# Queries and keys of a head pair leave PSUM in one cast and one subtraction; on-chip copies fill the stacks

## The chip, the core and the metric

The kernel runs on one core of one Trainium2 chip. Five engines work side by side, each through its own queue in order: PE (TensorE, matrix products), DVE (VectorE) and ACT (ScalarE) for elementwise work, POOL (GpSimd), and SP (SyncE), which here only issues DMA transfers. They wait for one another through semaphores. The metric is the time of one execution on the device in microseconds (us).

## The reference

One layer of a decoder: a half-step feed-forward block, two attention branches over one input projection, their gated sum, and a second half-step feed-forward block. Sequence 512, width 1024, everything in float32.

```python
x = x + 0.5 * swiglu_ffn(x, g1, wg1, wu1, wd1)
h = rms_norm(x, mix_norm)
(fq, fk, fv, ff, dq, dk, dv, iq, ik, iw, ga, gb) = split_columns(h @ w_in)
fq = rms_norm(fq.reshape(B, S, 8, 64), fox_q_norm)     # per head
fk = rms_norm(fk.reshape(B, S, 8, 64), fox_k_norm)
o_a = fox_attention(fq, fk, fv, log_sigmoid(ff + b_forget))
dq = rms_norm(dq.reshape(B, S, 8, 64), dsa_q_norm)
dk = rms_norm(dk, dsa_k_norm)                          # one key head for all
o_b = dsa_attention(dq, dk, dv, iq, ik, iw, rel_bias)  # top-128 keys
x = x + (sigmoid(ga) * (o_a @ wa) + sigmoid(gb) * (o_b @ wb)) @ w_out
x = x + 0.5 * swiglu_ffn(x, g2, wg2, wu2, wd2)
```

Branch A (FoX) has 8 query heads and 8 key heads of 64 columns. Branch B (DSA) has 8 query heads and one shared key head.

## The kernel before

Matrix products are made from two parts of each float32 number, a rounded high part (dtype fp32r) and the rest, the low part: high = cast(x), low = x - high. A product is the sum of three such products (`mm3`, lines 132 to 135). For the scores of attention there is a shorter form, since a head has only 64 columns and the array has 128 rows. A *stack* holds the high part of a head's queries in 64 partitions and the low part in the other 64, for all 512 positions. The keys lie twice, in `kh` (high, in both halves) and `kl` (low, in both halves). Two products, stack by `kh` and stack by `kl` (`stack_mm`, lines 651 and 652), then give all four terms.

The sequence of work in the middle part of the kernel is a loop over 16 heads `g`: 0 to 7 are FoX, 8 to 15 DSA. Each head has four beats `s`, one for each block of 128 queries, from the last block to the first. In a beat PE turns a block column of probabilities of the head before (`flip`, line 924: transposes into the PSUM bank `pt`; ACT casts it into `ph`, line 928, and DVE subtracts into `pl`, line 929), weighs values with it (`weigh`, lines 934 and 935, into `po`), makes the scores of the present block (`ps_qk`), and then a fixed amount of projection products (`ps_t`, `ps_f`) as filling. DVE adds the bias to the scores and takes the minimum (line 913), ACT takes the exponential (line 915), POOL divides (line 917). Between these DVE also makes steps of a top-128 search (`topk`, lines 861 to 866), which may only stand behind anchors: the instructions handed to `mark`.

Queries and keys of a pair of heads are prepared during the odd head ahead of the pair: `get_q(g + 1)` in beat 0 and, for FoX, `get_k(g + 1)` in beat 1. Four transposes (line 626) bring the 128 columns of both heads to the partitions of one PSUM bank, `ps_q` or `ps_k`: the even head in partitions 0 to 63, the odd head in 64 to 127. Both banks come from the tag `pt` with two buffers, which the transposes of line 924 use too. `split_own` then treats each head by itself: ACT scales and casts 64 partitions (line 645), DVE subtracts 64 partitions (line 646), and for queries these two write straight into the two halves of the head's stack, `st`. For keys the two parts of a head are written to the head's own half, and SP copies each to the other half by a DMA (line 978). The keys are the tiles `kh` and `kl`, three buffers each; the stacks have two buffers.

SP's queue carries, in order, the weight loads (line 122), the copies of keys (line 978) and the bias tile of the next head, `cb` (line 984: a row of cumulative forget sums spread over 128 partitions; two buffers, so that the load for head g + 1 waits until head g - 1 has read its own). The order of PE is the order of the program; the order of the other queues is set by a scheduler that simulates the kernel.

The function `evac_split` (lines 608 and 609), which casts and subtracts 128 partitions at once, is used for the shared key head of branch B.

## Time and profile before

| | us |
|---|---|
| median of 3 runs (1090.44 to 1095.73) | 1091.22 |
| the profiled execution | 1087.2 |
| its span, from the first to the last instruction | 1085.5 |

| engine | busy us | share of the span | instructions |
|---|---|---|---|
| PE, matrix products | 1069.2 | 99% | 6880 |
| DVE | 794.6 | 73% | 1286 |
| ACT | 575.9 | 53% | 908 |
| POOL | 194.4 | 18% | 248 |

How to read it: times in rows are microseconds from the start of the span. In a timeline row the first number is the start, the second the duration; in brackets stands how long the engine sat idle before the instruction and what released it. The queries and keys are prepared between 417 and 618 us. The granted clock of PE is 1.00 in every stretch of this time.

### The profile page before, as it was taken

Reading aid. Unit: us, or ns where it says so; the run is one execution under the profiler, and the core shown is the slowest. Engines: PE = TensorE matmul, PEld = TensorE weight load, DVE = VectorE, ACT = ScalarE, POOL = GpSimd, SP = SyncE. Lnnn points to the kernel's source line nnn. Section 1 sums busy time; section 2 is a strip of 40 time slices with the busy share of each in tenths; the row PEclk is TensorE's granted clock in tenths of the full one; section 3 lists DMA queues with packets and bytes.
Section 4 is the critical chain, followed back from the end, with each engine's and each line's share of the span. In section 5 each row is a group of like instructions: output and inputs, shape, how many; then the busy total and the mean of one; then the engine's idle time right before and its main releaser. Section 6 shows DMA issues by size and latency. Waiting matters only on the chain.

```text
span 1085.5 us, 17835 instructions
## 1 busy us (share of the span) xinstructions
PE 1069.2 (99%) x6880; PEld 966.8 (89%) x6880; DVE 794.6 (73%) x1286; ACT 575.9 (53%) x908; POOL 194.4 (18%) x248
## 2 busy tenths in 40 slices
PE   9999999999999999998999999999999999999998
PEld 7889899988998899988878778889998899989997
DVE  6895578755967489879665765879986688865874
ACT  5553155522555676887655685455663155522650
POOL 0000000000001415565552640001110001000100
PEclk9999999999999999999999999999999999999999
DMA  7434325533442368765124221425574356633552
GB/s 244 115 98 135 108 87 148 138 96 98 115 118 85 104 128 189 184 157 117 58 65 135 80 68 40 144 83 152 140 166 141 89 136 161 161 97 101 143 126 78
DMA packets 43573, 131.01 MB, mean 121 GB/s; under 512 B 5337, under 2 KB 5721, under 8 KB 43489
## 3 DMA queue, kind: packets, MB, share of 16 engines
q1 hardware_dynamic: 35120, 107.58, 32.4%
q0 software_dynamic: 8208, 22.02, 11.9%
q8 instruction: 54, 0.88, 0.3%
q10 hardware_dynamic: 160, 0.28, 0.1%
q14 instruction: 31, 0.25, 0.1%
HBM read 117.79 MB, written 2.11 MB: 110 GB/s over the span
## 4 chain that ended last, share of the span: by engine, by line
PE 86%; DVE 5%; DMA 3%; ACT 2%; issue 2%; POOL 2%; SPq 0%; DVEq 0%; POOLq 0%; ACTq 0%
PE pd L133 7%; PE pd L135 7%; PE pd L134 7%; PE pB L133 5%; PE pB L135 5%; PE pB L134 5%; PE pC L133 3%; PE pA L133 3%; PE pA L134 3%; PE pC L135 3%; PE pC L134 3%; PE pA L135 3%; PE ps_f L133 3%; PE ps_f L134 3%; PE ps_f L135 3%; DMA cb<-cum_rows 2%
## 5 line engine op out<-in xcount | busy, mean ns | idle before, releaser
L134 PE MATMUL pd<-al,wh 128*128 128x512 f32 (+1 forms) x294 | 113.2, 385 | 0.0
L133 PE MATMUL pd<-ah,wh 128*128 128x512 f32 (+1 forms) x294 | 113.2, 385 | 0.0
L135 PE MATMUL pd<-ah,wl 128*128 128x512 f32 (+1 forms) x294 | 113.1, 385 | 0.0
L112 ACT CAST wh<-s 128x1024 fp32r<-128x1024 f32 x57 | 60.1, 1055 | 98.6 <-PE pB L134 48.4
L133 PE MATMUL pB<-tbh,wh 128*128 128x256 f32 x304 | 85.0, 279 | 0.2 <-DVE u L435 0.2
L134 PE MATMUL pB<-tbl,wh 128*128 128x256 f32 x304 | 84.8, 279 | 0.0
L135 PE MATMUL pB<-tbh,wl 128*128 128x256 f32 x304 | 84.7, 279 | 0.0
L133 PE MATMUL ps_t<-wh,xh 128*128 128x256 f32 (+1 forms) x288 | 81.0, 281 | 0.0
L134 PE MATMUL ps_t<-wl,xh 128*128 128x256 f32 (+1 forms) x288 | 80.3, 279 | 0.0
L135 PE MATMUL ps_t<-wh,xl 128*128 128x256 f32 (+1 forms) x288 | 80.3, 279 | 0.0
L113 DVE TENSOR_TENSOR wl<-s,wh 128x1024 fp32r<-128x1024 f32 x57 | 69.4, 1217 | 1.8 <-ACT wh L112 1.7
L271 POOL DMA_DIRECT2D al<-gu x26 | 22.3, 858 | 260.7 <-ACT al L270 248.6
L135 PEld LDWEIGHTS pd<-ah,wl 128*128 128x128 f32 x294 | 55.3, 188 | 11.1
L134 PEld LDWEIGHTS pd<-al,wh 128*128 128x128 f32 x294 | 55.2, 188 | 10.9
L133 PEld LDWEIGHTS pd<-ah,wh 128*128 128x128 f32 x294 | 55.2, 188 | 10.8
L393 POOL DMA_DIRECT2D s<-in_w_pair_dram x11 | 9.7, 879 | 296.1 <-DVE wl L113 296.1
L133 PEld LDWEIGHTS pB<-tbh,wh 128*128 128x128 f32 x304 | 57.1, 188 | 0.6 <-issue 0.6
L134 PEld LDWEIGHTS pB<-tbl,wh 128*128 128x128 f32 x304 | 57.2, 188 | 0.0
L135 PEld LDWEIGHTS pB<-tbh,wl 128*128 128x128 f32 x304 | 57.1, 188 | 0.0
L133 PEld LDWEIGHTS ps_t<-wh,xh 128*128 128x128 f32 x288 | 54.3, 189 | 0.5
L134 PEld LDWEIGHTS ps_t<-wl,xh 128*128 128x128 f32 x288 | 54.3, 189 | 0.5
L135 PEld LDWEIGHTS ps_t<-wh,xl 128*128 128x128 f32 x288 | 54.3, 188 | 0.0
(354 smaller groups left out, 3597.0 us busy)
## 6 DMA issues: line engine op xcount, KB each, us to landing
rc<-in_w_pair_dram SPq DMA_DIRECT2D x16, 512.0 KB, 3.6
rb<-in_w_pair_dram SPq DMA_DIRECT2D x16, 512.0 KB, 3.6
ra<-in_w_pair_dram SPq DMA_DIRECT2D x15, 512.0 KB, 3.6
rd<-in_w_pair_dram SPq DMA_DIRECT2D x15, 512.0 KB, 3.7
re<-in_w_pair_dram SPq DMA_DIRECT2D x14, 512.0 KB, 3.8
al<-gu POOLq DMA_DIRECT2D x26, 256.0 KB, 4.7
s<-in_w_pair_dram POOLq DMA_DIRECT2D x11, 512.0 KB, 5.5
ra<-in_w_down_dram SPq DMA_DIRECT2D x7, 512.0 KB, 3.6
```

What stands on the lines that cost most here:

```text
L112: S.copy(wh[:, :f], raw[:, :f])
L113: V.tensor_sub(wl[:, :f], raw[:, :f], wh[:, :f].bitcast(F32))
L133: PE.matmul(out, lh, rh, start=start, stop=False, **more)
L134: PE.matmul(out, lh, rl, start=False, stop=False, **more)
L135: PE.matmul(out, ll, rh, start=False, stop=stop, **more)
L271: G.dma_start(l, u, accum_op=OP.add)
L393: G.dma_start(t["s2"], load["b"][2], accum_op=OP.add)
```

## The change

For the first pair (g = 0) nothing changes but the order of allocation. For the seven other pairs of queries and the three other pairs of FoX keys, one cast and one subtraction over 128 partitions (`evac_split`) replace two of each over 64. [...] For queries the high parts go to the even head's stack, all 128 partitions of it, and the low parts to a scratch tile `low` from the pool `tmp` (six buffers); three copies of 64 partitions then bring the odd head's high part to its stack, the even head's low part into the second half of the even stack, over the odd head's high part, and the odd head's low part into the odd stack. The copy into the second half of the even stack must wait until the copy that reads that half has landed. For keys both parts go to the even head's tiles; for each of `kh` and `kl` two copies bring the odd head's half to both halves of the odd tile, and a third brings the even head's half over it. That third copy waits for the first two.

```diff
             out = [at.tile([P, T], F32R, tag=tag, bufs=2, name="st") for tag in ("qh", "ql")]
-            for hf, st in enumerate(out):
-                own, oth = sides(hf)
-                split_own(ps, gain, own, st[own], st[oth])
+            if g == 0:
+                for hf, st in enumerate(out):
+                    own, oth = sides(hf)
+                    split_own(ps, gain, own, st[own], st[oth])
+                return out
+            even, odd = out
+            low = tmp_tile("low").bitcast(F32R)
+            evac_split(ps, gain, even, low)
+            copy_half(odd[0:DH], even[DH:P])
+            copy_half(even[DH:P], low[0:DH])
+            copy_half(odd[DH:P], low[DH:P])
             return out
+
+        def copy_half(dst, src):
+            nc.sync.dma_start(dst.bitcast(F32), src.bitcast(F32))
...
-            out = []
-            for hf in range(2):
-                own, oth = sides(hf)
-                k = [mp.tile([P, T], F32R, tag=tag, bufs=3, name=tag) for tag in ("kh", "kl")]
-                split_own(ps, hg[:, 2:3], own, k[0][own], k[1][own])
-                for t in k:
-                    nc.sync.dma_start(t[oth].bitcast(F32), t[own].bitcast(F32))
-                out.append(k)
+            out = [[mp.tile([P, T], F32R, tag=tag, bufs=3, name=tag) for tag in ("kh", "kl")] for _ in range(2)]
+            if g == 0:
...
+            evac_split(ps, hg[:, 2:3], *out[0])
+            for even, odd in zip(*out):
+                for part in (slice(0, DH), slice(DH, P)):
+                    copy_half(odd[part], even[DH:P])
+                copy_half(even[DH:P], even[0:DH])
             return out
```

PE's instructions and their order stay the same. ACT and DVE have 10 casts and 10 subtractions fewer; SP has 43 copies in place of 16.

SP's queue while the pair of heads 2 and 3 is prepared, before. `kh_4747` and `kl_4748` are the even head's keys, `kh_4753` and `kl_4754` the odd head's; `cb_4901` is the bias of head 3.

```order
L122 DMA rb_5064<-in_w_dq_dram 128x1024
L978 DMA kh_4747<-kh_4747 64x512
L978 DMA kl_4748<-kl_4748 64x512
L978 DMA kh_4753<-kh_4753 64x512
L978 DMA kl_4754<-kl_4754 64x512
L122 DMA rc_5244<-in_w_dq_dram 128x1024
L984 DMA cb_4901<-cum_rows_3396 128x512
```

The same place of SP's queue after the change: `st_4692` is the even stack, `st_4693` the odd one, `kh_4749` and `kl_4750` are the even keys, `kh_4751` and `kl_4752` the odd ones.

```order
L122 DMA rb_5066<-in_w_dq_dram 128x1024
L975 DMA st_4693<-st_4692 64x512
L975 DMA st_4693<-low_4694 64x512
L975 DMA st_4692<-low_4694 64x512
L975 DMA kh_4751<-kh_4749 64x512 x2
L975 DMA kl_4752<-kl_4750 64x512 x2
L975 DMA kh_4749<-kh_4749 64x512
L975 DMA kl_4750<-kl_4750 64x512
L1000 DMA cb_4903<-cum_rows_3396 128x512
L122 DMA rc_5248<-in_w_dq_dram 128x1024
```

Nine copies stand where four stood, the copies that complete the even keys are the last of them, and the bias of head 3 has moved ahead of the weight load.

SP's queue at the pair of heads 6 and 7, before; `cb_5747` is the bias of head 7.

```order
L978 DMA kh_5617<-kh_5617 64x512
L978 DMA kl_5618<-kl_5618 64x512
L978 DMA kh_5623<-kh_5623 64x512
L978 DMA kl_5624<-kl_5624 64x512
L984 DMA cb_5747<-cum_rows_3396 128x512
```

And after; the even keys are `kh_5623` and `kl_5624`, `cb_5753` is the bias of head 7.

```order
L975 DMA st_5565<-st_5564 64x512
L975 DMA st_5565<-low_5566 64x512
L975 DMA st_5564<-low_5566 64x512
L975 DMA kh_5625<-kh_5623 64x512 x2
L975 DMA kl_5626<-kl_5624 64x512 x2
L975 DMA kh_5623<-kh_5623 64x512
L1000 DMA cb_5753<-cum_rows_3396 128x512
L975 DMA kl_5624<-kl_5624 64x512
```

The load of the bias, which waits until head 5 has read the tile's old content for the last time, now stands ahead of the copy that completes the even head's low keys.

DVE's queue at beat 0 and 1 of head 1, where the pair of heads 2 and 3 is prepared, as one piece of the difference. `st`, `low` and `kl` are the subtractions, `pl` that of the probabilities, the rows of lines 861 and 863 are steps of the search.

```order
-L646 SCALAR_TENSOR_TENSOR st<-ps_q,gq,st 64x512
+L609 SCALAR_TENSOR_TENSOR low<-ps_q,gq,st 128x512
+L863 MATCH_REPLACE sc_3400<-m_4709,sc_3400 128x512
+L861 MAX m_4772<-sc_3398 128x8
 L929 TENSOR_TENSOR pl<-pt,ph 128x512
 L616 TENSOR_REDUCE ss<-sqh 128x8
 L916 RECIPROCAL rs<-rs 128x1
+L609 SCALAR_TENSOR_TENSOR kl<-ps_k,hg,kh 128x512
+L863 MATCH_REPLACE sc_3398<-m_4772,sc_3398 128x256
+L861 MAX m_4823<-sc_3399 128x8
 L617 TENSOR_SCALAR ss<-ss 128x8
-L646 SCALAR_TENSOR_TENSOR st<-ps_q,gq,st 64x512
```

The subtraction that frees the bank `ps_q` is done once and early (its second half stood below `L617`, the last row here); two steps of the search, anchored on it, now stand ahead of `pl`, and the subtraction of the keys stands ahead of where its first half stood.

## The prediction

> **What bounds the kernel now.** I read the page first: busy time by engine, and the chain of work that ended last.

> ```profile
> PE 1069.2 (99%) x6880; PEld 966.8 (89%) x6880; DVE 794.6 (73%) x1286; ACT 575.9 (53%) x908; POOL 194.4 (18%) x248
> PE 86%; DVE 5%; DMA 3%; ACT 2%; issue 2%; POOL 2%; SPq 0%; DVEq 0%; POOLq 0%; ACTq 0%
> ```

> PE is busy for 99% of the span. The change takes no product away, so it can only gain PE's idle time (1085.5 - 1069.2 = 16 us, part of it at the start) or add to it. Casts and subtractions saved on ACT and DVE count only where PE waited for them. Next I read who waited for whom on PE, over the attention alone (440 to 660 us):

> ```profile
> PE pt L924 <- DVE pl L929: 1.9, 3, 0.9
> PE pt L924 <- DVE rs L916: 1.7, 2, 0.9
> PE po L935 <- DVE pl L929: 1.6, 3, 1.0
> PE pt L924 <- DVE st L646: 1.5, 2, 1.0
> PE po L934 <- DVE o L947: 1.1, 3, 0.7
> PE ps_q L626 <- POOL kn L724: 0.8, 1, 0.8
> PE pt L924 <- POOL p L917: 0.6, 2, 0.3
> PE ps_k L626 <- DVE pl L929: 0.6, 2, 0.3
> ```

> The numbers are the total, the count and the longest. All eight rows sum to 9.8 us, 0.9% of the time: this is the whole that a change to these evacuations could win, and only 1.5 us stand on the subtraction of queries itself.

> **What is removed.** The price of each old instruction, and of the new ones, which the kernel already uses once for the shared key (the numbers behind the count are the least, the median and the greatest duration in ns):

> ```profile
> L645 ACT ACTIVATE st<-ps_q,gq x16: 674/683/687, 429.7 to 617.0; 64x512 fp32r<-64x512 f32 x16
> L646 DVE SCALAR_TENSOR_TENSOR st<-ps_q,gq,st x16: 743/750/756, 431.9 to 617.9; 64x512 fp32r<-64x512 f32 x16
> L608 ACT ACTIVATE dkh<-ps_dk,hg x1: 674/674/674, 420.9 to 420.9; 128x512 fp32r<-128x512 f32 x1
> L609 DVE SCALAR_TENSOR_TENSOR dkl<-ps_dk,hg,dkh x1: 729/729/729, 423.0 to 423.0; 128x512 fp32r<-128x512 f32 x1
> ```

> 128 partitions cost what 64 cost. So seven pairs of queries and three of keys save 10 x 0.68 = 6.8 us of ACT and 10 x 0.75 = 7.5 us of DVE. Nearly all of it lies beside PE's work. What reaches PE is the bank: `ps_q` is free after one subtraction instead of two, and the transposes of the next beat find it free.

> For branch B the banks then alternate strictly: the transposes of beat 2 wait for `low` and no longer for the `pl` of the beat before. Its waits behind an evacuation are these:

> ```profile
> 534.04 0.52 PE L924 MATMUL pt<-ident,p 128*128 128x128 f32 x3 [0.77 <-DVE rs L916]
> 558.34 0.55 PE L924 MATMUL pt<-ident,p 128*128 128x128 f32 x3 [0.92 <-DVE pl L929]
> 559.54 0.50 PE L934 MATMUL po<-ph,dvv 128*128 128x512 f32 x1 [0.65 <-DVE o L947]
> L913 DVE CUSTOM_DVE_ANT_0 p<-ps_qk,b 128x384 f32<-128x384 f32 x6 | 3.3, 550 | 0.1
> ```

> At 534 (pair 8) the transposes gain up to 0.77, but the product with `pl` two instructions later needs the same `pl`, so I take 0.6. At 558 (pair 10) 0.92 goes, and what is late next is `po`, which waits for `o`; the scheduler has moved `o` ahead of one score block (0.55, last row), so 0.6 of the 1.57 goes. Pairs 12 and 14 show nothing of this size. **Branch B: -1.2 us** (bounds 0 and -2.3, the three waits).

> **What is added: a chain of copies.** The old evacuation of queries needed no DMA. Now the even stack is complete only after ACT's cast, a first copy, and a second one that waits for the first to land. For keys each copy was independent; now the even keys need copies to the odd tile first, then one more. The price of a copy from its issue to its landing, in the three stretches where FoX keys are copied (the row of the `kl` copies, then the landing of all four):

> ```profile
> L978 SPq DMA_DIRECT2D kl<-kl x2: 461/464/467, 454.2 to 455.8; - x2
> DMA to landing us min/median/max: 2.2/4.3/4.6
> L978 SPq DMA_DIRECT2D kl<-kl x2: 461/462/462, 482.8 to 485.3; - x2
> DMA to landing us min/median/max: 2.2/2.2/4.2
> L978 SPq DMA_DIRECT2D kl<-kl x2: 461/464/467, 510.7 to 513.0; - x2
> DMA to landing us min/median/max: 2.2/2.4/3.9
> ```

> A copy takes 2.2 us alone, and up to 4.6 when other transfers are in flight; issuing one holds SP for 0.46. Bounds per copy: 2.2 and 4.6.

> Queries have room. The tightest pair is the last:

> ```profile
> 613.99 0.60 PE L626 MATMUL ps_q<-ident,kn 128*128 128x128 f32 x4
> 622.63 0.39 PE L651 MATMUL ps_qk<-dkh,st 128*128 128x512 f32 x1
> ```

> Between the end of the transposes and the first use lie 8.0 us; the cast and two copies take 0.7 + 2 x 2.2 = 5.1, or 6.7 at 3.0 each. I cost the query copies at nothing; the cover is the filling products of that head, and it is gone from 3.6 us a copy on.

> Keys are made one beat later and have less. Here are the end points, for pairs 2, 4 and 6 in turn: the transposes or the subtraction that start the chain, and the product that uses the even low keys (pair 4: also a weight load and the last copy on SP; pair 6: the score block on DVE and the load of the bias):

> ```profile
> 450.67 0.63 PE L626 MATMUL ps_k<-ident,kn 128*128 128x128 f32 x4 [0.29 <-DVE pl L929]
> 459.67 0.40 PE L652 MATMUL ps_qk<-kl,st 128*128 128x512 f32 x1
> 482.02 0.74 DVE L646 SCALAR_TENSOR_TENSOR kl<-ps_k,hg,kh 64x512 fp32r<-64x512 f32 x1
> 484.58 0.33 SPq L122 DMA_DIRECT2D rc<-in_w_ga_dram  x1
> 485.27 0.46 SPq L978 DMA_DIRECT2D kl<-kl  x1
> 488.09 0.39 PE L652 MATMUL ps_qk<-kl,st 128*128 128x512 f32 x1
> 513.18 0.29 DVE L913 CUSTOM_DVE_ANT_0 p<-ps_qk,cb 128x128 f32<-128x128 f32 x1
> 513.57 0.62 SPq L984 DMA_DIRECT2D cb<-cum_rows  x1
> 515.64 0.39 PE L652 MATMUL ps_qk<-kl,st 128*128 128x512 f32 x1
> ```

> Let t be the time of one copy.

> Pair 2: `ps_k` is complete at 451.3, less the 0.29 that it waited. Cast and subtraction (0.67 + 0.73) and two handovers end at 452.9. The two copies of `kl` to the odd tile leave SP at 453.0 and 453.5, the second lands at 453.5 + t, and the last copy at 453.6 + 2t. With t = 3.6, between the least and the greatest here, that is 460.8: **1.1 us** after the present use at 459.67. The chain takes the place of the 1.0 us wait for `st`, which goes.

> Pair 4: the first subtraction ends at 482.8 today; with the second query subtraction gone but two search steps moved ahead of the scores, I leave it at 482.2. The copies leave at 482.4 and 482.9. One lands after 2.2. The last one leaves at 485.2, just behind a weight load of 512 KB, as today's last copy does, which took 4.2. So 489.4, **1.3 us** after 488.09.

> Pair 6: the scheduler has put the bias load ahead of the last `kl` copy. That load waits until head 5's last score block has read the old bias (513.18 + 0.29). SP issues the load at 513.57 and can issue the copy only at 514.2. With 2.6 for it, 516.8: **1.2 us** after 515.64.

> Who waits: PE, at the first product of heads 2, 4 and 6, with everything behind it. Behind the waiting copies on SP stand the bias of a later head and weight loads. The bias waits for the end of its head anyway, so it loses less than 1 us, and at pair 2 it gains its place ahead of a weight load; the weights have at least a beat in hand. I cost these at nothing; if a bias lands later, POOL and the softmax behind it add that lateness to the head.

> **What is absorbed.** A late PE finds its next waits shorter, where others set them. The next ones behind pairs 2, 4 and 6:

> ```profile
> 475.99 0.44 PE L626 MATMUL ps_q<-ident,kn 128*128 128x128 f32 x2 [0.82 <-POOL kn L724]
> 490.93 0.66 PE L924 MATMUL pt<-ident,p 128*128 128x128 f32 x4 [0.35 <-POOL p L917]
> 526.81 0.39 PE L935 MATMUL po<-pl,fv 128*128 128x256 f32 x1 [0.34 <-DVE pl L929]
> ```

> The first two hang on POOL, which is paced by its own queue and the biases that it waits for; the third on DVE, which now has less to do. I take all three as swallowed: 0.8, 0.35 and 0.35.

> **Sum** against the profiled execution, 1087.2: pair 2 +1.1 - 0.8 = +0.3; pair 4 +1.3 - 0.35 = +0.95; pair 6 +1.2 - 0.35 = +0.85; branch B -1.2. Together +0.9, so 1088.1. The median of the runs shown, 1091.22, stands 4.0 above the profiled execution; in its terms the forecast is 1092.1. About 0.5% (5.5 us) is what a measurement of this kernel can tell from no change, so this is within it.

> With one t for all key copies the same sum reads (2t - 6.9) + (2t - 5.4) + (t - 1.8) - 1.2 = 5t - 15.3, until a pair has no stall left.

> [...]

> **The rivals.**
> Copies land in time. Every copy takes 2.2 us, as the medians of pairs 4 and 6 nearly do. Pair 2 completes its keys at 458.0 and pair 4 at 487.4, before their use; their gains are mostly lost again in the waits that POOL sets, so about 0 each. Pair 6 still ends at 516.4, +0.4 after its absorption. With branch B -0.8: 1086.4, or 1090.4. For it: the copies could ride in quiet stretches. Against it: pair 2 runs beside a 512 KB load that POOL issues, and nine copies now follow each other.

> Slower, by the copies' contention. More copies in a row, with weight loads and POOL's loads beside them, push every copy to 4.6: 5 x 4.6 - 15.3 = +7.7, hence 1098.9. It decides from t = 4.2 on, where the sum passes +5.5. For it: the median at pair 2 is 4.3. Against it: at pairs 4 and 6 it is 2.2 and 2.4.

> Faster by relief. DVE is the engine behind most of the waits on PE; with 7.5 us fewer on it, waits elsewhere in the attention could shrink too. To pass 5.5 us it would have to clear over half of the 9.8 us and leave no stall on keys: 1085.

> **How the numbers follow.** Forecast (near balance, 1089.5 to 1096) 0.58; in time 0.21; slower by contention 0.16; relief 0.05. The first two lie within 0.5%, which makes 0.79; faster 0.05, slower 0.16. The range reaches from the in-time case with branch B at its bound and a gain of about 1 us kept at pairs 2 and 4 (1090.4 - 1.1 - 1.1 = 1088.2), 1088, to the contention case with the longest copy of the trace, 1099.

> **What would show it.** PE's waits should show new rows at lines 651 and 652 for a DMA of `kl`, `kh` or `st`, 1 to 3 us long, at the start of heads 2, 4 and 6 and nowhere else; the wait for `st` on line 924 gone; ACT and DVE 7 us less busy; the last `kl` copy of pair 6 issued right behind the bias. The forecast is wrong if heads 8 to 14 begin with such a wait, if the key copies take other than 2.2 to 4.6 us, or if PE's waits for POOL grow because a bias lands late.

## The result and the profile after

| | before | after |
|---|---|---|
| median of the runs, us | 1091.55 (4 runs) | 1105.3 (4 runs, 1102.18 to 1106.43) |
| ratio to before, 95% interval | | 1.0114 (1.008 to 1.0148) |
| the profiled execution, us | 1087.2 | 1102.18 |
| its span, us | 1085.5 | 1100.5 |

The change costs 1.1%. The forecast was 1092.1 with a range to 1099; the time lies outside it, on the slow side. The profiled execution is 15.0 us longer than that of before.

The page of the changed kernel: busy time of each engine with its share of the span.

```profile
PE 1074.9 (98%) x6880; PEld 971.7 (88%) x6880; DVE 785.1 (71%) x1276; ACT 569.2 (52%) x898; POOL 194.1 (18%) x248
```

DVE is 9.5 us and ACT 6.7 us less busy, where 7.5 and 6.8 were worked out. But the same 6880 products keep PE busy for 5.7 us longer (1069.2 before), and its idle time rose from 16.3 to 25.6 us, by 9.3. These two make the 15.0. First the idle time: the two largest rows of PE's waits over the attention (440 to 660 us; total, count, longest).

```profile
PE ps_qk L651 <- DMA kh<-kh: 6.1, 2, 4.9
PE ps_qk L652 <- DMA kl<-kl: 4.6, 3, 2.5
```

The wait for `st` on line 924 (1.5 us before) is gone, and 10.7 us of waits for copies of keys have come. PE's timeline shows where: the first two rows at head 2, the next two at head 4, the last at head 6.

```profile
461.32 0.50 PE L651 MATMUL ps_qk<-kh,st 128*128 128x512 f32 x1 [1.21 <-DMA kh<-kh]
461.98 0.50 PE L652 MATMUL ps_qk<-kl,st 128*128 128x512 f32 x1 [0.16 <-DMA kl<-kl]
496.25 0.49 PE L651 MATMUL ps_qk<-kh,st 128*128 128x512 f32 x1 [4.88 <-DMA kh<-kh]
498.70 0.79 PE L652 MATMUL ps_qk<-kl,st 128*128 128x512 f32 x1 [1.96 <-DMA kl<-kl]
530.60 0.67 PE L652 MATMUL ps_qk<-kl,st 128*128 128x512 f32 x1 [2.51 <-DMA kl<-kl]
```

Most of it, 6.84 us, stands at head 4. SP's queue there, in the changed kernel (start, time that issuing held the queue):

```profile
481.27 0.47 SPq L975 DMA_DIRECT2D st<-st  x1
482.06 5.56 SPq L975 DMA_DIRECT2D st<-low  x2
487.71 1.19 SPq L975 DMA_DIRECT2D kh<-kh  x2
488.99 1.19 SPq L975 DMA_DIRECT2D kl<-kl  x2
490.70 0.46 SPq L975 DMA_DIRECT2D kh<-kh  x1
491.21 0.58 SPq L122 DMA_DIRECT2D rc<-in_w_ga_dram  x1
492.31 1.32 SPq L975 DMA_DIRECT2D kl<-kl  x1
493.73 0.54 SPq L1000 DMA_DIRECT2D cb<-cum_rows  x1
```

The copies from the stack to the odd stack and from `low` are the queries'. The second row holds two of them: one leaves at 482.06, the other overwrites what the first copy still reads, and leaves only when that has landed. All that SP has to issue stands behind it. ACT's row for the high keys of this pair, and DVE's for the low keys:

```profile
484.39 0.69 ACT L608 ACTIVATE kh<-ps_k,hg 128x512 fp32r<-128x512 f32 x1
485.11 0.75 DVE L609 SCALAR_TENSOR_TENSOR kl<-ps_k,hg,kh 128x512 fp32r<-128x512 f32 x1 [0.42 <-ACT kh L608]
```

The high keys are ready at 485.08, and their first copy leaves at 487.71: 2.6 us in the queue. The low keys are ready at 485.86, and their first copy leaves at 488.99, 3.1 us later. How long this pair's copies took to land, first those of `st`, then those of `kh` (least, median, most):

```profile
DMA to landing us min/median/max: 2.2/4.0/5.9
```

```profile
DMA to landing us min/median/max: 2.3/2.3/5.5
```

The 5.9 is the first query copy (481.27 to 487.15, where the waiting one leaves). The 5.5 is the one that completes the even `kh`: it leaves at 490.70 and lands at 496.2, where PE's wait ends. The copy that completes the even `kl` took longer still; the chain of work that ended last shows it (start, length), and PE's second wait ends behind it:

```profile
492.31 6.35 DMA kl<-kl
```

Now the longer busy time. Windows of PE behind the three waits (from:to, length, busy time and instructions, granted clock, DMA share, GB/s):

```profile
462.50:465.50 3.00, 3.00 (x16) 0.50 0.86 171
496.60:503.20 6.60, 4.64 (x21) 0.50 0.23 69
530.80:534.10 3.30, 3.30 (x16) 0.50 0.00 0
535.00:540.00 5.00, 5.00 (x35) 1.00 0.00 0
```

Behind each of the three waits the granted clock is 0.50 for some 3.4 or 6.8 us, 13.65 us together. PE is idle for 1.96 us of them, within the second wait of head 4, and busy for 11.7 (3.00 + 4.64 + 3.30 = 10.9 in these windows, 0.75 at their edges). Nearly all that PE does there is `ps_t` products, which follow one another every 0.213 us (499.72 to 502.92 us, 15 steps); at a clock of 1.00 they follow every 0.117 (535.73 to 537.25, 13 steps). By this ratio an estimated 5.3 of the 11.7 us are lost, most of the 5.7. Before, the clock was 1.00 throughout this stretch. The profiled execution is the fastest of the four; the other three had a mean granted clock of 0.989 to 0.992 where it had 0.994, so slow stretches took more of their time.

### The profile page after: what moved, and what is told of

It reads as the page before. It is cut to its first block, busy times and chain, and to the rows that moved or that the text cites. A ratio compares the mean times of both kernels' runs of the same rounds, so it can differ in the third digit from the quotient of the medians.

```text
span 1100.5 us, 17863 instructions
## 1 busy us (share of the span) xinstructions
PE 1074.9 (98%) x6880; PEld 971.7 (88%) x6880; DVE 785.1 (71%) x1276; ACT 569.2 (52%) x898; POOL 194.1 (18%) x248
## 4 chain that ended last, share of the span: by engine, by line
PE 88%; DMA 4%; DVE 3%; ACT 2%; issue 1%; POOL 1%; SPq 0%; DVEq 0%; ACTq 0%; POOLq 0%
PE pd L133 7%; PE pd L134 7%; PE pd L135 7%; PE pB L133 5%; PE pB L135 5%; PE pB L134 5%; PE pC L133 3%; PE pC L135 3%; PE pA L133 3%; PE pA L134 3%; PE pC L134 3%; PE pA L135 3%; PE ps_f L133 3%; PE ps_f L134 3%; PE ps_f L135 3%; PE ps_t L133 2%
## 5 line engine op out<-in xcount | busy, mean ns | idle before, releaser
L134 PE MATMUL ps_t<-wl,xh 128*128 128x256 f32 (+1 forms) x288 | 82.6, 287 | 0.0
L135 PEld LDWEIGHTS pd<-ah,wl 128*128 128x128 f32 x294 | 55.2, 188 | 11.1
L133 PEld LDWEIGHTS pd<-ah,wh 128*128 128x128 f32 x294 | 55.2, 188 | 10.9
L134 PEld LDWEIGHTS pd<-al,wh 128*128 128x128 f32 x294 | 55.2, 188 | 10.7
L134 PEld LDWEIGHTS ps_t<-wl,xh 128*128 128x128 f32 x288 | 56.6, 196 | 0.6
L133 PEld LDWEIGHTS ps_t<-wh,xh 128*128 128x128 f32 x288 | 56.6, 196 | 0.4
L915 ACT ACTIVATE p<-p,mn 128x512 f32<-128x512 f32 (+1 forms) x64 | 36.0, 562 | 40.1 <-DVE mn L913 39.7
```

The costliest lines, as they stand in the source:

```text
L133: PE.matmul(out, lh, rh, start=start, stop=False, **more)
L134: PE.matmul(out, lh, rl, start=False, stop=False, **more)
L135: PE.matmul(out, ll, rh, start=False, stop=stop, **more)
L915: S.activation(p, p, AF.Exp, bias=mn, scale=-1.0, accum_out=rs)
```

## The experiments

Three candidate causes: the keys' own chain of two landings, the queries' waiting copy ahead of the keys on SP, and the mere number of copies with their contention. Beside them the question whether the clock falls because of the waits. Unless said otherwise each experiment is an edit of the changed kernel. The first four ran beside one another on a chip (before: 1090.75 us), so did the next four (1090.73) and the last two (1090.32).

| experiment | median us | ratio to before (95%) | profiled: waits for copies of keys or queries at heads 2, 4, 6 | time at half clock, 446 to 560 us |
|---|---|---|---|---|
| the change | 1105.3 | 1.0114 (1.008 to 1.0148) | 10.7 | 13.7 |
| keys alone | 1104.47 | 1.0123 (1.0105 to 1.014) | 11.1 | 13.7 |
| queries alone | 1091.29 | 1.0012 (0.9995 to 1.003) | 0 | 6.8 |
| PE kept busy | 1096.63 | 1.007 (1.0048 to 1.0092) | 0.5 | 0 |
| chain on the odd head | 1097.18 | 1.006 (1.0041 to 1.0078) | 1.0 | 13.7 |
| keys, no chain | 1089.81 | 0.9997 (0.9988 to 1.0006) | 0 | 0 |
| keys first | 1095.47 | 1.0046 (1.0029 to 1.0063) | 9.0 | 6.8 |
| waiting copies last | 1086.57 | 0.9962 (0.9951 to 0.9974) | 0 | 0 |
| branch B's queries alone | 1089.11 | 0.9984 (0.9974 to 0.9994) | 0 | 0 |
| queries alone, waiting copy last | 1087.8 | 0.9969 (0.9957 to 0.9982) | 0 | 0 |
| keys alone, waiting copies last | 1092.57 | 1.0023 (1.0009 to 1.0037) | 0.8 | 3.4 |

Medians of different groups are compared by their ratios to before. Two profiles, branch B's queries alone and queries alone with the waiting copy last, have besides a stretch of 3.4 us at half clock from 422 us on, ahead of the stretch of the last column and behind no wait of PE (last section).

### Keys alone

```diff
 def get_q(g):
-            if g == 0:
+            if True:
```

Every pair of queries then goes the old way: two blocks of 64 partitions and no copies.

> Keys in the new way (one block, six copies, the last two in a chain), queries in the old way for all pairs, so that no query copy stands in SP's queue. Theory (the queue and the chain share the loss): the keys are ready earlier after their projection than in the changed kernel; TensorE waits 1 to 2 us for key tiles at heads 2, 4 and 6 each, less than the 10.7 us in all of the changed kernel, and the clock halves after one or two of the waits: 1093 to 1099 us. Rival (the query copies are the whole cause): no wait over 0.5 us, 1091 us. Rival (the keys' chain is the whole cause): as the changed kernel, 1104 to 1106 us.

1104.5 us: all of the loss, with no query copy on SP. The waits, then SP's queue at pair 2, then how long the three `kl` copies of that pair took to land:

```profile
PE ps_qk L652 <- DMA kl<-kl: 10.9, 3, 6.1
```

```profile
454.52 0.46 SPq L975 DMA_DIRECT2D kl<-kl  x1
455.48 0.55 SPq L975 DMA_DIRECT2D kh<-kh  x1
456.08 0.93 SPq L975 DMA_DIRECT2D kl<-kl  x1
457.10 0.54 SPq L122 DMA_DIRECT2D rc<-in_w_dq_dram  x1
460.47 0.46 SPq L975 DMA_DIRECT2D kl<-kl  x1
```

```profile
DMA to landing us min/median/max: 4.4/4.7/6.0
```

The copies to the odd tile leave at 454.5 and 456.1. The one that completes the even keys may leave when they have landed, at 460.5, and lands 6.0 us later, beside a weight load of 512 KB issued at 457.1 and another that POOL issues. PE waits for it from 460.4 to 466.5. So the keys' chain is enough by itself, as the last of the expectations had it.

### Queries alone

```diff
 def get_k(g):
-            if g == 0:
+            if True:
```

Every pair of keys then goes the old way: two blocks and four copies that wait for none.

> Queries in the new way (one block, three copies, the third waits for the first), keys in the old way for all pairs (two blocks of 64 partitions, four copies). Theory (the waiting query copy holds SP's queue, and the key copies stand behind it): the old key copies are ready when they were before but leave late at pair 4, so TensorE waits 1 to 3 us for the key tiles there and little at pairs 2 and 6; a clock loss of 0 to 3 us comes on top, and branch B gives back some 0.5 us: 1092 to 1098 us where the kernel before takes 1091.5. Rival (the keys' own chain of two landings is the whole cause, the queries cost nothing): no wait for key tiles, clock 1.00, 1091 us or less.

1091.3 us, within the interval of no change: between the two expectations, and the wait is not where either put it. PE's row, and POOL's row behind it, in the profiled execution:

```profile
496.49 1.11 PE L924 MATMUL pt<-ident,p 128*128 128x128 f32 x4 [5.58 <-POOL p L917]
```

```profile
495.79 0.29 POOL L1006 TENSOR_SCALAR_AFFINE_SELECT cb<-cb 128x128 f32<-128x128 f32 x1 [7.69 <-DMA cb<-cum_rows]
```

SP's queue in the same place (the first row is again two copies, the second of which waits):

```profile
479.04 5.82 SPq L975 DMA_DIRECT2D st<-low  x2
488.03 0.58 SPq L1000 DMA_DIRECT2D cb<-cum_rows  x1
```

The waiting query copy held SP for 5 us, and what came late was the bias of head 5, for which POOL waited 7.7 us and PE, through the probabilities, 5.6. The keys were in time. The place in the queue is only part of the lateness: the bias left SP 2.1 us later than before (485.97 there) and then took 7.6 us to land in place of 4.1. So the waiting copy does harm to what stands behind it, and something in this version pays it back (below).

### PE kept busy

```diff
             ps = psum.tile([P, T], F32, tag="s", bufs=2, name="ps_qk")
+            if i == NT - 1:
+                for _ in range({2: 8, 4: 30, 6: 12}.get(g, 0)):
+                    PE.matmul(ps, xh[0][:, 0:P], xh[1], start=True, stop=True)
```

> The changed kernel, with 8, 30 and 12 dummy products of 128x128 by 128x512 put ahead of the first scores of heads 2, 4 and 6, into the bank that those scores then overwrite, so that TensorE works through the time in which it waited. Theory (the waits halve the granted clock for 3.4 to 6.8 us behind them): the waits at the first scores fall below 1 us in all, the granted clock is 1.00 throughout, and the time is that of the changed kernel less 4 to 7 us, 1098 to 1101 us. Rival (the slow products come from something other than the wait ahead of them): the clock falls to 0.5 at the same places, 1104 us or more.

The dummy products are overwritten by the first scores. PE's wait for a copy, and its window over heads 2 to 7:

```profile
PE ps_qk L652 <- DMA kl<-kl: 0.5, 2, 0.3
```

```profile
440.00:545.00 105.00, 100.60 (x719) 1.00 0.58 139
```

The clock is 1.00 (over the whole execution too), and the time falls to a ratio of 1.007, 0.0044 or 4.8 us less than the change (about 0.4 to 9.2, from the two intervals). The 50 products fill the waits with work that nobody needs, so the time of the waits is still lost. 1096.6 us is a little below the 1098 to 1101 expected. That these three waits make the slow products behind them is shown by the clock; the size, 5.3 us, is worked out from the windows above.

### The chain on the odd head

```diff
-            evac_split(ps, gain, even, low)
-            copy_half(odd[0:DH], even[DH:P])
+            evac_split(ps, gain, odd, low)
+            copy_half(even[0:DH], odd[0:DH])
             copy_half(even[DH:P], low[0:DH])
-            copy_half(odd[DH:P], low[DH:P])
+            copy_half(odd[0:DH], low[DH:P])
...
-            evac_split(ps, hg[:, 2:3], *out[0])
+            evac_split(ps, hg[:, 2:3], *out[1])
             for even, odd in zip(*out):
                 for part in (slice(0, DH), slice(DH, P)):
-                    copy_half(odd[part], even[DH:P])
-                copy_half(even[DH:P], even[0:DH])
+                    copy_half(even[part], odd[0:DH])
+            for _, odd in zip(*out):
+                copy_half(odd[0:DH], odd[DH:P])
```

> The changed kernel with the two parts of the pair exchanged: the evacuations write the odd head's tiles, the even head gets copies of one landing, and the chained copies fall to the odd head, which is wanted a head later. Number, size and kind of the instructions and copies stay. Theory (what the even head waits for sets the loss): the even head's key tiles are whole one landing, 2.3 us, earlier; waits fall by 1 to 2.3 us at each of heads 2, 4 and 6, pair 4 still waits since the waiting query copy holds the queue: 1094 to 1101 us. Rival (the number of copies, and their contention with the weight loads, costs the time): 1104 to 1106 us as the changed kernel.

1097.2 us: about 6 us regained with the same copies (1.0114 to 1.006). The waits for keys fall to 1.0, all of it at head 2; at head 4, where a wait was still expected, there is none. The longest wait left came through POOL, again by the bias, as PE's and POOL's rows show:

```profile
501.64 1.11 PE L924 MATMUL pt<-ident,p 128*128 128x128 f32 x4 [4.39 <-POOL p L917]
```

```profile
500.95 0.29 POOL L1007 TENSOR_SCALAR_AFFINE_SELECT cb<-cb 128x128 f32<-128x128 f32 x1 [6.72 <-DMA cb<-cum_rows]
```

The bias left SP at 494.26, behind nine copies, of which the waiting query copy alone held the queue until 489.3. It then took 6.6 us to land.

### Keys, no chain

The keys-alone run, with the block in two scratch tiles and eight copies that wait for none.

```diff
-            evac_split(ps, hg[:, 2:3], *out[0])
-            for even, odd in zip(*out):
-                for part in (slice(0, DH), slice(DH, P)):
-                    copy_half(odd[part], even[DH:P])
-                copy_half(even[DH:P], even[0:DH])
+            both = [tmp_tile(nm).bitcast(F32R) for nm in ("bh", "bl")]
+            evac_split(ps, hg[:, 2:3], *both)
+            for src, even, odd in zip(both, *out):
+                for part in (slice(0, DH), slice(DH, P)):
+                    copy_half(even[part], src[0:DH])
+                for part in (slice(0, DH), slice(DH, P)):
+                    copy_half(odd[part], src[DH:P])
```

> Keys alone in one block as in the run with the keys alone (queries in the old way), but the block goes to two tiles of its own, and eight copies of 64 partitions by 512 fill the four key tiles, none of which waits for another. Theory (the chain of two landings costs the time, not the number of copies): TensorE's waits for key tiles fall from 10.9 us to under 3, the clock stays at 1.00, 1090 to 1094 us. Rival (volume or contention: two copies more in each pair): at least the 1104.5 us of the run with the keys alone.

1089.8 us, no wait for keys, against 1104.5 with two copies fewer in a chain. The chain costs the time, not the number of copies.

### Keys first

```diff
-                    if s == 0 and g % 2:
-                        nq = get_q(g + 1)
-                    if s == 1 and g % 2:
-                        nk = get_k(g + 1)
+                    if s == 0 and g % 2:
+                        nk = get_k(g + 1)
+                    if s == 1 and g % 2:
+                        nq = get_q(g + 1)
```

> The changed kernel with the keys of the next pair made a beat earlier and the queries a beat later (their places exchanged), all else as changed. Theory (keys come late because their chain starts late and stands behind the queries' waiting copy): the keys are whole in time, and the queries' own waiting copy, in turn behind the key copies, now ends last: waits of 0 to 3 us at the first score for the query tile, 1092 to 1100 us. Rival (the number of copies costs the time): 1104 to 1106 us.

PE's waits, 440 to 660 us:

```profile
PE ps_qk L651 <- DMA st<-low: 10.5, 4, 5.5
```

Whichever is made last ends last: the even stack's waiting copy takes the keys' place, with 1.94, 5.53 and 1.54 us at heads 2, 4 and 6, more at head 4 than the 0 to 3 expected (the fourth, 1.5, stands at 630 us). Yet the time is 1095.5. Nearly the same waits as in the change lowered the clock for 6.8 us in place of 13.7: only the one at head 4 did.

### Waiting copies last

The run with the chain on the odd head, and the three copies that wait, all of them now the odd head's, are put behind the bias load of that head on SP (`later_copies` is the list of copies put off, `bias_load[0]` the load of the bias).

```diff
-            copy_half(odd[0:DH], low[DH:P])
+            later_copies.append((odd[0:DH], low[DH:P]))
...
-                copy_half(odd[0:DH], odd[DH:P])
+                later_copies.append((odd[0:DH], odd[DH:P]))
...
                     if s == 0:
                         nb = get_bias(g + 1)
+                    if s == 0 and g % 2 == 0:
+                        while later_copies:
+                            with tc.issue_after(bias_load[0].ins):
+                                copy_half(*later_copies.pop(0))
```

> The run with the two parts of the pair exchanged, and besides the three waiting copies (the odd head's low queries and the two that double the odd head's keys) leave SP behind the bias of the odd head, so that no bias, weight or key copy stands behind a wait for a copy. Theory (what stands behind a waiting copy, and the even head's second landing, make up the waits): no wait of TensorE over 1 us for a key tile or a bias at heads 2 to 7, granted clock 1.00, 1089 to 1092 us where the kernel before takes 1090.75. Rival (so many copies cost time by contention, wherever they stand): 1095 us or more.

1086.6 us, 0.38% (0.26 to 0.49) faster than the kernel before, and better than expected. All of PE's waits, 440 to 660 us, and SP's queue at pair 4:

```profile
PE po L935 <- DVE pl L929: 2.0, 4, 1.0
PE pt L924 <- DVE rs L916: 1.7, 2, 1.0
PE pt L924 <- DVE pl L929: 1.4, 3, 0.7
PE pt L924 <- POOL p L917: 1.3, 2, 1.0
PE po L934 <- DVE o L947: 1.2, 3, 0.8
PE ps_q L626 <- POOL kn L724: 0.8, 1, 0.8
```

```profile
482.55 1.11 SPq L977 DMA_DIRECT2D kh<-kh  x2
483.76 1.18 SPq L977 DMA_DIRECT2D kl<-kl  x2
485.25 0.33 SPq L122 DMA_DIRECT2D rc<-in_w_ga_dram  x1
486.76 0.33 SPq L1003 DMA_DIRECT2D cb<-cum_rows  x1
487.14 0.47 SPq L977 DMA_DIRECT2D st<-low  x1
487.71 0.54 SPq L977 DMA_DIRECT2D kh<-kh  x1
488.34 0.56 SPq L977 DMA_DIRECT2D kl<-kl  x1
```

The first key copy leaves at 482.55, when its data is there (ACT's cast ends at 482.5), the bias 7 us earlier than in the change (2.6 of them because the queries' copies begin earlier); the waiting copies come when nothing stands behind them that is wanted soon. The kernel has the change's 43 copies and its blocks, so their number is not what cost the time.

### Parts of this version

> Queries of all pairs in one block with their waiting copy put behind the bias of the odd head (as in the run with all waiting copies put back), keys in the old way. Theory (in the run with the queries alone, what they saved was given back where SP stood behind the waiting copy): the 5.6 us wait for POOL at pair 4 falls to about 1 us, clock 1.00, 1086 to 1089 us where the kernel before takes 1090.7 and the queries alone took 1091.3. Rival (that wait was of that one execution, not of the order of the queue): as the queries alone, 1090 to 1092 us.

> Keys of pairs 2, 4 and 6 in one block with the chained copies on the odd head, behind its bias; queries in the old way. Theory (the keys alone lost 13.7 us to their chain, and to nothing else): no wait over 1.2 us for key tiles, clock 1.00; six instructions of DVE and ACT go, of which the wait for the key block at 452 us gives back up to 1 us: 1088 to 1091 us. Rival (one block with copies costs time whatever the order): 1094 us or more.

> The new way for the queries of heads 8 to 15 alone; heads 0 to 7 as before. The profile of the changed kernel shows some 0.7 us less of TensorE's waits over heads 8 to 15, and no key copies are made there: 0 to 1.2 us less than the kernel before, 1089.5 to 1090.8 us, clock 1.00. Rival (copies on SP delay the weight loads of branch B): 1092 us or more.

The first two keep one half of the version above, the queries or the keys, and treat the other as before; the third is the change's way for the queries of heads 8 to 15 alone (`if g < H:` in place of `if g == 0:`). With the queries alone the waiting copy's place, together with the exchange of the two heads, is worth 0.43% or 4.7 us (ratios 1.0012 and 0.9969), and the wait for POOL at pair 4 falls from 5.6 to 1.4. This half holds the gain; the whole version (0.9962) can't be told from it. Branch B alone gains 1.6 us (0.7 to 2.8). The keys alone come out a little slower than before, against what was expected. PE's row at pair 4, and how long the bias of head 5 took to land:

```profile
494.82 0.80 PE L924 MATMUL pt<-ident,p 128*128 128x128 f32 x4 [3.63 <-POOL p L917]
```

```profile
DMA to landing us min/median/max: 7.4/7.4/7.4
```

It took 4.1 before. It left SP in time (486.57, before 485.97), so here only its flight was long. The copies beside it are not enough to explain that, since the whole version has them too and its bias took 4.8 us. The profiles point to POOL's next 512 KB weight load. In four of them the bias of head 5 left 0.6 us or more ahead of that load and landed in 4.1 to 5.1 us (before, branch B's queries alone, and both versions with the queries' waiting copy last). In five it left between 0.3 us ahead of the load and 0.9 behind it, and took 6.5 to 7.8 (this run, keys alone, queries alone, keys without a chain, chain on the odd head). In the other three it left 3 us or more behind the load and took 3.5 to 5.4. No run moves the load alone, so this is an order that was seen and not a cause that was shown.

## Why the prediction was wrong

- **Removed work, branch B.** Right. DVE and ACT lost 9.5 and 6.7 us; heads 8 to 14 begin without a wait for a copy; branch B's -1.2 stands against -1.6 in the changed kernel's trace (its waits at 534 and 558 us before, 0.77 and 0.92, are gone, and the one for `o` grew from 0.65 to 0.78) and -1.6 in the run with it alone.
- **Where the waits come.** Right: at heads 2, 4 and 6 and nowhere else, at lines 651 and 652; at pair 6 the bias stands ahead of the last copy, as foretold.
- **The sizes of the stalls, where the sum failed.** It had 1.1, 1.3 and 1.2 us; the trace has 1.37, 6.84 and 2.51. Two steps failed, the cost of standing behind a waiting copy and the price of a copy.
- **"I cost the query copies at nothing"**, and with it "I cost these at nothing" of what stands behind the waiting copies on SP. The working let the key copies leave when their data was ready; at pair 4 the `kh` copies left 2.6 us later, when SP was free, and the `kl` copies, behind them, 3.1 us later. I had asked what a waiting copy does to the user of its own data, to the bias and to the weights, but not to the six key copies next in the queue; and the bias did come late (queries alone: 5.6 us of PE, in part by its longer flight).
- **The price of a copy.** The last one in the chain was to take 3.6 at pair 2, 4.2 at pair 4 and 2.6 at pair 6, with 4.6 as the bound, the most that the trace before showed for copies that wait for none. Beside other loads copies took longer than that in these traces, whether they wait or not: at pair 4 the first query copy took 5.9, which is why the waiting one held SP so long, and the copy that completes `kl` took 6.35. At pair 6 the last copy took 4.2 (526.37 to 530.56). At pair 2 it took 2.3 in the change, but 6.0 in the run with the keys alone, whose PE waits 6.1 us there.
- **Pair 4 added up**, along `kl`. The copies were to leave 0.2 us after the subtraction and left 3.1 after it: 2.9. The last one was to leave 2.8 behind the first and left 3.3 behind it: 0.5. It was to take 4.2 and took 6.35: 2.2. Together 5.6, and 5.5 were missing (6.84 - 1.3).
- Which of the two weighs more depends on what else is there. Without the queries' copies the keys' chain alone still loses the whole 1.2%. With the chain off the even head, from 1.0114 to 1.006, the waiting copies in the queue still cost 1.0% (1.006 to 0.9962).
- **The clock, a term that was missing.** 5.3 us of the profiled 15.0, as worked out above. The text said that the clock was 1.00 and then costed a wait at its own length only.
- **Absorption.** Of the three next waits taken as swallowed, only the one behind pair 4 (0.35) is gone. The one for POOL behind pair 2 is still there, 0.93 us long at 480.08, and so is the one for `pl` behind pair 6, 0.34 at 543.42. So 1.15 of the 1.5 us were not absorbed: what PE waits for there comes later than before by 4.1 us (POOL's `kn`, 480.08 and 475.99) and 16.6 us (DVE's `pl`, 543.42 and 526.81), about as much as PE itself is late. No run shows what delays POOL and DVE there.

Stalls of 10.7 in place of 3.6 (+7.1), the clock (+5.3), what was not absorbed (+1.15) and what branch B gave beyond its term (-0.4) account for 13.2 of the 14.1 us by which the sum was short (15.0 - 0.9).

The rival "slower, by the copies' contention" named the right place and the right sign, at 1098.9, and got 0.16. Half of its own form held: copies beside weight loads took even longer than its 4.6, up to 6.35. The other half, that so many copies cost time by themselves, did not: with 43 copies and those that wait issued last, the time was 1086.6 us, 0.9962 of before.

## What to carry to other kernels

Here a DMA that waits for another one held its whole issuing queue, 5 us at pair 4; list what is queued behind it, and issue the waiting ones last, for the consumer that needs them last. Give the longer chain of a pair to the member that is used later. Cost a stall of TensorE at its length plus the slow stretch where one follows: here the stalls of 10.7 us at three heads took 5.3 us more by the reckoning above, while one of 1.94 us left the clock at 1.00.

## What the runs showed of the hardware

```profile
461.17 0.47 PE L651 MATMUL ps_qk<-kh,st 128*128 128x512 f32 x1 [1.94 <-DMA st<-low]
```

```profile
469.50 0.50 PE L935 MATMUL po<-pl,fv 128*128 128x512 f32 x1 [1.98 <-DVE pl L929]
```

The first left the clock at 1.00, the second was followed by 3.4 us at 0.50. In the profiles here single waits up to 1.17 us left the clock as it was, except in the change at pair 2, where 1.21 and 0.16 us within 1.9 us lowered it; between there and 1.98 both happened, and of the waits from 1.98 us on that stood in this stretch every one lowered it. The slow stretches lasted about 3.4 us or twice that, and the three of the change begin at 462.5, 496.6 and 530.8 us, each 34.1 us behind the last. One stood behind no stall: in the run with branch B's queries alone PE was busy without a gap from 405 us on, and the clock still fell at 422.3 (windows as above):

```profile
405.00:422.20 17.20, 17.20 (x152) 1.00 0.84 194
422.30:425.70 3.40, 3.40 (x17) 0.50 0.89 144
```

The run with the queries alone and their waiting copy last shows the same; before the change the clock was 1.00 there. No run shows why, so not every slow stretch of these kernels can be put down to a wait.
